# A hybrid decoder layer: the state-space preparation in 21 held phases, later right-hand weights on the way back, the second gate/up stage in program order

## The chip, the cores and the metric

One Trainium2 chip, one core of it. The metric is device microseconds for one execution of the whole layer.

## The reference

One decoder layer on 1024 rows of width 1024, all in float32: half a step of a SwiGLU feed-forward, a mixing layer, another half step of SwiGLU. `D_FF` is 2816, in 22 blocks of 128.

```python
def swiglu(h, w_gate, w_up, w_down):
    return (jax.nn.silu(h @ w_gate) * (h @ w_up)) @ w_down

mod = c_act @ w_ada[l] + b_ada[l]          # 9 vectors of 1024: shift, scale, gate of three sub-layers
h = modulate(rms_norm(x, g_pre_ff1[l]), sh1, sc1)
x = x + 0.5 * ga1 * rms_norm(swiglu(h, w1_gate[l], w1_up[l], w1_down[l]), g_post_ff1[l])
h = modulate(rms_norm(x, g_pre_mix[l]), sh2, sc2)
proj = h @ w_in[l]                         # q, k, v for attention, u for the state-space part
attn = sliding_window_attention(q, k, v, attn_sinks[l])
ssm = s5_ssm(u, ssm_a_re[l], ...)          # powers of lam_bar = exp(dt*lam), B_bar, C: tables from parameters alone
mixed = concat(rms_norm(attn, g_attn_out[l]), rms_norm(ssm, g_ssm_out[l])) @ w_out[l]
x = x + ga2 * rms_norm(mixed, g_post_mix[l])
h = modulate(rms_norm(x, g_pre_ff2[l]), sh3, sc3)
x = x + 0.5 * ga3 * rms_norm(swiglu(h, w2_gate[l], w2_up[l], w2_down[l]), g_post_ff2[l])
```

## The kernel before

Every large product is float32 made of three float32r matmuls (`mm3`, L74 to L76: high by high, high by low, low by high). `split` makes the halves: ScalarE copies the high one (L69), VectorE subtracts for the low one (L70). On top of that the products are Strassen's: sums and differences of quadrants, computed on VectorE, replace one product in eight.

The stages follow each other on TensorE:

- The first gate/up stage (`g1`, to 517 us). It begins with quadrant products whose results are combined in `first_done`; then `rest` runs 140 products of 12 matmuls, seven (1, 5, 6, 2, 7, 3, 4) for each 128-block of the gate or up weights. `rest` converts the weights of the product after the next (`wt.conv(i + 3)`), runs the product (`step`) and calls a hook (`hook1(i)`). After a product ScalarE copies its bank into a buffer `h` (L468, L470, L472) or VectorE adds to one (L464, L456); the fourteenth product of a pair of blocks ends in four sums (`sums`, L427, into four `h` buffers), which are stored in DRAM (`g_d`) for the way back.
- The first way back (`down(0)`, 517 to about 690 us), 66 products of `PRODUCTS` over `NH_F` = 11 blocks: `load` fetches the stored left operand and, for products 1 and 2, the weight pair L and R; `sums` forms differences of weights (L530, L532, L535, L537); `conv` splits both operands. Loads run seven products ahead. Its hook is `hook2(s)`.
- The mixing layer (to about 1040 us), the second gate/up stage (`g2`, to 1517) and the second way back (`down(2)`), the same code as the first two. `g2` computes its `sums` on POOL (GpSimd), `g1` on DVE (VectorE).

A list scheduler with estimated times decides the order of each engine's instructions. Three things bind it: `pinned(f)` chains what `f` issues to the previous pinned instruction of the same engine; `tc.keep_in_program_order` holds one instruction; `g1.rest` gets `pinned`, `g2.rest` gets a function that pins nothing.

Three jobs lie beside the products. The modulation vectors are 72 blocks: a load of 512 KB and one VectorE multiply-and-reduce (`ada_block`, L164, 128x1024; `ada_half`, L169, half of one). 40 of them run in `hook1` until about product 60, 16 halves in `hook2`, 8 in `hook3`. `gate_row` and `gate_store` (L177, L183) turn a vector of gates into a row through TensorE. And the preparation of the state-space part, `prep_steps`, returns 12 steps; `hook1` calls one each at the products of `prep_at`, not pinned; what is left over is called in `hook2`. Its last eight are `step_e` and `step_f` for four q: VectorE rows L1207 to L1215, TensorE transposes L1235 and small products L1270.

## Time and profile before

| | |
|---|---|
| median of 3 runs | 1730.32 us (1730.04 to 1730.64) |
| the profiled execution | 1733.73 us, span 1732.0 us, mean granted clock 0.983 |
| TensorE (PE) busy | 1663.4 us, 96% |
| VectorE (DVE) busy | 1261.8 us, 73% |
| ScalarE (ACT) busy | 813.1 us, 47% |
| GpSimd (POOL) busy | 201.4 us, 12% |
| DMA | 249 MB, mean 144 GB/s |

A group row reads: line, engine, operation, output<-inputs, shapes, xcount, then busy time and mean nanoseconds of one, then the engine's idle time ahead of it and what ended that. A row of waits reads: engine, line that waited <- engine and line waited for: total us, times, longest. A timeline row: start us, duration of the run of like instructions, engine, line, operation, count. A row of a stretch reads: from:to, its length, then busy time (and count) of PE, PE's weight loads, DVE, ACT and POOL, then the clock that TensorE was granted (1 is full), the share of the 16 DMA engines, and GB/s. A busy PE is not PE at its peak: the count in a stretch says more.

### The profile page before, as it was taken

Reading aid. Unit: us, or ns where it says so; the run is one execution under the profiler, and the core shown is the slowest. Engines: PE = TensorE matmul, PEld = TensorE weight load, DVE = VectorE, ACT = ScalarE, POOL = GpSimd, SP = SyncE. Lnnn points to the kernel's source line nnn. Section 1 sums busy time; section 2 is a strip of 40 time slices with the busy share of each in tenths; the row PEclk is TensorE's granted clock in tenths of the full one; section 3 lists DMA queues with packets and bytes.
Section 4 is the critical chain, followed back from the end, with each engine's and each line's share of the span. In section 5 each row is a group of like instructions: output and inputs, shape, how many; then the busy total and the mean of one; then the engine's idle time right before and its main releaser. Section 6 shows DMA issues by size and latency. Waiting matters only on the chain.

```text
span 1732.0 us, 22199 instructions
## 1 busy us (share of the span) xinstructions
PE 1663.4 (96%) x7669; PEld 1358.0 (78%) x7669; DVE 1261.8 (73%) x2426; ACT 813.1 (47%) x1656; POOL 201.4 (12%) x208
## 2 busy tenths in 40 slices
PE   5999999999998999899989998989999999999998
PEld 4878887778886888788767886868888888888886
DVE  7989998995569758826489378785665555687586
ACT  5633335534334457835575257723333333344562
POOL 0011100120010000000013044021211111110001
PEclk8999999999999999999999998999999999999999
DMA  9176742453298342500143126152332223394334
GB/s 377 38 269 228 260 162 104 157 169 105 73 367 281 109 123 101 193 25 25 55 121 94 47 75 197 71 182 101 101 127 98 98 97 109 107 393 139 106 105 160
DMA packets 111041, 249.08 MB, mean 144 GB/s; under 512 B 12088, under 2 KB 27744, under 8 KB 110928
## 3 DMA queue, kind: packets, MB, share of 16 engines
q1 hardware_dynamic: 99776, 209.40, 35.4%
q0 software_dynamic: 10576, 37.21, 6.3%
q8 instruction: 60, 0.98, 0.2%
q10 hardware_dynamic: 576, 1.05, 0.2%
q14 instruction: 53, 0.43, 0.1%
HBM read 187.87 MB, written 59.75 MB: 143 GB/s over the span
## 4 chain that ended last, share of the span: by engine, by line
PE 49%; DVE 6%; issue 1%; ACT 1%; DMA 1%; POOL 0%; DVEq 0%; SPq 0%; ACTq 0%; POOLq 0%
PE b L75 14%; PE b L76 14%; PE b L74 14%; DVE a L70 1%; PE b L743 1%; PE b L831 1%; PE b L833 1%; PE b L832 1%; PE b L777 1%; ACT a L69 1%; PE b L922 0%; PE b L203 0%; DMA w<-in_w_out 0%; DVE w L70 0%; PE b L918 0%
## 5 line engine op out<-in xcount | busy, mean ns | idle before, releaser
L74 PE MATMUL b<-a,w 128*128 128x512 f32 x1260 | 494.0, 396 | 13.6 <-ACT h L468 7.4
L75 PE MATMUL b<-a,w 128*128 128x512 f32 x1260 | 496.3, 394 | 5.2 <-DVE a L70 5.2
L76 PE MATMUL b<-a,w 128*128 128x512 f32 x1260 | 494.1, 395 | 4.7 <-DVE w L70 4.7
L74 PEld LDWEIGHTS b<-a,w 128*128 128x128 f32 x1260 | 240.3, 191 | 67.1 <-ACT h L468 9.6
L76 PEld LDWEIGHTS b<-a,w 128*128 128x128 f32 x1260 | 240.0, 190 | 57.5 <-DVE w L70 6.9
L75 PEld LDWEIGHTS b<-a,w 128*128 128x128 f32 x1260 | 240.1, 191 | 56.5 <-DVE a L70 6.6
L70 DVE TENSOR_TENSOR w<-r,w 128x512 fp32r<-128x512 f32 (+1 forms) x206 | 153.8, 748 | 104.9 <-ACT w L69 103.9
L75 PE MATMUL b<-w,r 128*128 128x512 f32 x528 | 205.1, 391 | 5.9 <-DVE w L70 5.6
L69 ACT CAST w<-r 128x512 fp32r<-128x512 f32 (+1 forms) x210 | 130.5, 625 | 161.7 <-PE b L76 93.6
L76 PE MATMUL b<-w,r 128*128 128x512 f32 x528 | 203.7, 390 | 0.4 <-DVE r L70 0.4
L74 PE MATMUL b<-w,r 128*128 128x512 f32 x528 | 176.5, 390 | 0.8 <-ACT w L69 0.4
L69 ACT CAST r<-a 128x512 fp32r<-128x512 f32 x110 | 68.3, 623 | 151.9 <-PE b L76 84.6
L70 DVE TENSOR_TENSOR r<-a,r 128x512 fp32r<-128x512 f32 x110 | 77.6, 706 | 73.6 <-ACT r L69 72.0
L75 PEld LDWEIGHTS b<-w,r 128*128 128x128 f32 x528 | 99.1, 188 | 30.2 <-DVE w L70 9.7
L464 DVE TENSOR_TENSOR h<-h,b 128x512 f32<-128x512 f32 x120 | 82.1, 686 | 52.9 <-PE b L76 50.3
L74 PEld LDWEIGHTS b<-w,r 128*128 128x128 f32 x528 | 98.9, 188 | 22.2 <-ACT w L69 0.9
L76 PEld LDWEIGHTS b<-w,r 128*128 128x128 f32 x528 | 99.0, 188 | 21.0 <-DVE r L70 0.8
L70 DVE TENSOR_TENSOR w<-t,w 128x512 fp32r<-128x512 f32 (+1 forms) x114 | 79.8, 700 | 47.2 <-ACT w L69 47.1
L427 POOL TENSOR_TENSOR h<-h,h 128x512 f32<-128x512 f32 x44 | 71.0, 1624 | 305.5 <-DVE h L456 303.9
L69 ACT CAST w<-t 128x512 fp32r<-128x512 f32 (+1 forms) x114 | 70.1, 615 | 67.4 <-DVE t L335 28.4
L70 DVE TENSOR_TENSOR w<-a,w 128x512 fp32r<-128x512 f32 x110 | 77.3, 703 | 3.8 <-ACT w L69 3.8
L69 ACT CAST w<-a 128x512 fp32r<-128x512 f32 x110 | 67.9, 618 | 16.4 <-PE b L76 7.2
(378 smaller groups left out, 2586.7 us busy)
## 6 DMA issues: line engine op xcount, KB each, us to landing
r<-in_w_gu SPq DMA_DIRECT2D x88, 512.0 KB, 4.1
g_d<-h SPq DMA_DIRECT2D x154, 256.0 KB, 2.1
a<-g_d SPq DMA_DIRECT2D x110, 256.0 KB, 2.8
q<-in_w_ada POOLq DMA_DIRECT2D x48, 512.0 KB, 4.6
a<-in_w_d SPq DMA_DIRECT2D x88, 256.0 KB, 5.4
a<-in_w_ada SPq DMA_DIRECT2D x16, 512.0 KB, 10.2
a<-in_x SPq DMA_DIRECT2D x12, 512.0 KB, 6.6
x_d<-a SPq DMA_DIRECT2D x12, 512.0 KB, 3.6
```

What stands on the lines that cost most here:

```text
L69: act.copy(hi, src)
L70: eng.tensor_tensor(lo, src, hi.bitcast(F32), op=SUB)
L74: pe.matmul(psum, wh, xh, start=first, stop=False, skip_group_check=goes_on)
L75: pe.matmul(psum, wh, xl, start=False, stop=False, skip_group_check=goes_on)
L76: pe.matmul(psum, wl, xh, start=False, stop=last, skip_group_check=goes_on)
L427: self.eng.tensor_tensor(d, x, y, op=op)
L464: dve.tensor_tensor(dst, dst, pb, op=ADD)
L743: pe.matmul(pb[kv][:, m % 2, ks], qT[m][rows, t * P : (t + 1) * P], kT[rows, (t + 1 - nk) * P : (t + 1) * P], start=True, stop=True,)
L777: pe.transpose(pt[:, m, :], pr[4 * kv + m][:, b * P : (b + 1) * P], ident)
L831: pe.matmul(pb, hh, wh, start=k == 0, stop=False)
L832: pe.matmul(pb, hh, wl, start=False, stop=False)
L833: pe.matmul(pb, hl, wh, start=False, stop=k == NK - 1)
```

## The change

- `pinned` gets `hold`: with `hold=False` an instruction stands behind the pinned ones ahead of it, and later pinned ones need not follow it.
- `prep_steps` becomes `prep_phases`, a generator of 21 phases. `hook1` runs the next phase, pinned with `hold=False`, at each product i with i % 7 in (2, 5) once the modulation blocks are done: products 61, 65, 68 and so on to 131. The first loads and is followed by a pinned `gate_store(0)`; 65 to 79 are the exponentials, angles, powers and kr/bb; 82 to 100 are the turn tables, in three steps each with two sets of buffers; 103 to 131 are e and f, each part's small products a phase behind its VectorE part. What `hook2` would drain is then empty.
- In both ways back the right-hand weights are loaded `LAG` = 4 products later than the left, and their difference (L530) is formed four products later.
- `hook2` begins the late modulation halves at product 26 (loads) and 30 (the reduction), before at 18 and 22; their loads go from POOL's queue to SP's, in program order, as does the load of c.
- `g2.rest` and `hook3` are pinned. `hook3` begins its 8 blocks at products above 8 instead of 3, and stores the gate row at 44 instead of 40.
- `sums` runs on DVE in both gate/up stages. Two single holds in the preparation go.

```diff
-    def pinned(f, *args):
+    def pinned(f, *args, hold=True):
...
-            last_of[i.engine] = i
+            if hold:
+                last_of[i.engine] = i
...
-                self.eng.tensor_tensor(d, x, y, op=op)
+                dve.tensor_tensor(d, x, y, op=op)
...
+    LAG = 4
...
-                    L[i], R[i] = slot(f"a{i}", [2, 512]), slot(f"a{16 + i}", [2, 512])
-                for h, x in enumerate((L, R)):
-                    tc.keep_in_program_order(sp.dma_start(x[i][:, c], wd[i, c, :, h]))
+                    L[i] = slot(f"a{i}", [2, 512])
+                tc.keep_in_program_order(sp.dma_start(L[i][:, c], wd[i, c, :, 0]))
+            if LAG <= s < 2 * NH_F + LAG:
+                c, i = divmod(s - LAG, NH_F)
+                if c == 0:
+                    R[i] = slot(f"a{16 + i}", [2, 512])
+                tc.keep_in_program_order(sp.dma_start(R[i][:, c], wd[i, c, :, 1]))
...
-            if m == "2":
-                dve.tensor_tensor(R[i][:, 0], R[i][:, 1], R[i][:, 0], op=SUB)
-            elif m == "6":
+            k = s - NH_F - LAG
+            if 0 <= k < NH_F:
+                dve.tensor_tensor(R[k][:, 0], R[k][:, 1], R[k][:, 0], op=SUB)
+            if m == "6":
...
-        steps = [step_base, lambda: two(step_tw, 0), lambda: two(step_tw, 2)]
+        yield from step_base()
+        for q in range(6):
+            yield
+            for f, k in ((tw_store, q - 2), (tw_turns, q - 1), (tw_angles, q)):
+                if 0 <= k < 4:
+                    f(k)
         parts = [f(q) for q in range(4) for f in (step_e, step_f)]
-        steps.append(parts[0][0])
-        for i in range(1, 8):
-            steps.append(lambda i=i: (parts[i - 1][1](), parts[i][0]()))
-        steps.append(parts[7][1])
-        return steps
+        for i in range(9):
+            yield
+            if i > 0:
+                parts[i - 1][1]()
+            if i < 8:
+                parts[i][0]()
...
-        elif prep and i == prep_at[0]:
-            prep_at.pop(0)
-            prep.pop(0)()
-            if len(prep_at) == 10:
-                gate_store(0)
+        elif prep and i % 7 in (2, 5):
+            pinned(next, prep[0], None, hold=False)
+            if not stored:
+                pinned(gate_store, 0)
+                stored.append(0)
...
-        elif s >= 2 * NH_F - 4:
+        elif s >= 2 * NH_F + 4:
             if not late_c:
-                late_c.append(load_c(pool))
+                late_c.append(load_c(sp))
...
-                pool.dma_start(w, a["w_ada"][j][:, 512 * h : 512 * h + 512])
+                tc.keep_in_program_order(sp.dma_start(w, a["w_ada"][j][:, 512 * h : 512 * h + 512]))
...
-            if s >= 2 * NH_F and late_raw:
+            if s >= 2 * NH_F + 8 and late_raw:
...
-        if last_raw and i > 3 and i % 2:
+        if last_raw and i > 8 and i % 2:
...
         if i == 40:
             gate_row(2, 8, True)
+        if i == 44:
             gate_store(2)
 
-    g2.rest(hook3, lambda f, *args: f(*args))
+    g2.rest(lambda i: pinned(hook3, i), pinned)
```

The orders that follow are those of one engine. A row is the line, the operation, output<-inputs and the shape; the lines of the changed kernel are 2 higher from L113 on, 8 higher from L526 on and 14 to 16 higher in the preparation (L169 is L171 there, L183 L185, L427 L429, L464 L466, L530 L538, L1207 L1221, L1270 L1284).

VectorE in `g1.rest`, before, ahead of the converted weight (`w_430`) of about product 86, where four sums stand among preparation rows (L1207 to L1210 of e or f, L1291 and L1292 of the turn tables):

```order
L335 TENSOR_TENSOR t_428_2807<-r_400_2594,r_399_2592 128x512
L1291 TENSOR_SCALAR q_418_2723<-q_417_2722 128x512
L1208 TENSOR_TENSOR q_440_2887<-q_355_2151,q_356_2152 128x512
L456 TENSOR_TENSOR h_404_2645<-h_404_2645,b_406_2650 128x512
L1292 TENSOR_TENSOR q_417_2722<-q_417_2722,q_418_2723 128x512
L427 TENSOR_TENSOR h_412_2699<-h_381_2486,h_404_2645 128x512
L427 TENSOR_TENSOR h_407_2663<-h_404_2645,h_384_2505 128x512
L427 TENSOR_TENSOR h_410_2682<-h_407_2663,h_381_2486 128x512
L1207 TENSOR_TENSOR q_438_2885<-q_355_2151,q_356_2152 128x512
L1210 TENSOR_TENSOR q_439_2886<-q_355_2151,q_356_2152 128x512
L427 TENSOR_TENSOR h_429_2822<-h_386_2522,h_410_2682 128x512
L70 TENSOR_TENSOR w_430_2831<-t_428_2807,w_430_2831 128x512
```

The changed kernel's VectorE ahead of the converted weight of product 114 (`w_509`), with rows of the phase at 110 (L1221 to L1229) and the four sums behind product 111 (L429). From the row behind the converted weight of 112 to this one there are 18 rows, of which these are the last 12; the first of the 18 is the last that needs nothing of product 110:

```order
L70 TENSOR_TENSOR w_506_3408<-r_471_3176,w_506_3408 128x512
L337 TENSOR_TENSOR t_507_3411<-r_472_3178,r_471_3176 128x512
L1293 SCALAR_TENSOR_TENSOR c_502_3395<-delta,cols,c_502_3395 128x16
L458 TENSOR_TENSOR h_479_3238<-h_479_3238,b_481_3243 128x512
L1223 TENSOR_TENSOR q_503_3399<-q_503_3399,q_505_3401 128x512
L429 TENSOR_TENSOR h_487_3292<-h_461_3111,h_479_3238 128x512
L429 TENSOR_TENSOR h_482_3256<-h_479_3238,h_464_3130 128x512
L1225 TENSOR_TENSOR q_505_3401<-q_356_2169,q_357_2170 128x512
L429 TENSOR_TENSOR h_485_3275<-h_482_3256,h_461_3111 128x512
L1229 TENSOR_TENSOR q_504_3400<-q_504_3400,q_505_3401 128x512
L429 TENSOR_TENSOR h_508_3426<-h_466_3147,h_485_3275 128x512
L70 TENSOR_TENSOR w_509_3435<-t_507_3411,w_509_3435 128x512
```

The turn-table rows are gone from among the sums, and rows of one part are left there.

VectorE at the start of the first way back, before (L169 are the modulation halves, each with a readout row):

```order
L70 TENSOR_TENSOR w_661_4309<-a_643_4214,w_661_4309 128x512
L169 ISA h_708_4609,modc<-h_708_4609,c_707_4606,cols 128x512
L169 ISA modc 128x1
L169 ISA h_709_4611,modc<-h_709_4611,c_707_4606,modc 128x512
L169 ISA modc 128x1
L70 TENSOR_TENSOR r_666_4352<-a_648_4224,r_666_4352 128x512
L169 ISA h_710_4613,modc<-h_710_4613,c_707_4606,cols 128x512
L169 ISA modc 128x1
L70 TENSOR_TENSOR w_667_4353<-a_649_4226,w_667_4353 128x512
L169 ISA h_711_4615,modc<-h_711_4615,c_707_4606,modc 128x512
L169 ISA modc 128x1
L70 TENSOR_TENSOR r_669_4375<-a_653_4248,r_669_4375 128x512
```

And in the changed kernel, the splits there (of `r` the left operand, of `w` the weights) and the first sums:

```order
L70 TENSOR_TENSOR w_669_4389<-a_605_4114,w_669_4389 128x512
L70 TENSOR_TENSOR r_675_4418<-a_653_4282,r_675_4418 128x512
L70 TENSOR_TENSOR w_676_4419<-a_607_4118,w_676_4419 128x512
L538 TENSOR_TENSOR a_612_4128<-a_612_4128 128x512
L540 TENSOR_TENSOR a_601_4104<-a_601_4104,a_612_4128 128x512
L543 TENSOR_TENSOR t_748_4874<-a_612_4128,a_601_4104 128x512
```

No half stands among these splits. Some twenty products on:

```order
L70 TENSOR_TENSOR w_740_4812<-a_635_4202,w_740_4812 128x512
L171 ISA h_732_4781,modc<-h_732_4781,c_731_4778,cols 128x512
L171 ISA modc 128x1
L70 TENSOR_TENSOR r_742_4832<-a_721_4701,r_742_4832 128x512
L171 ISA h_733_4783,modc<-h_733_4783,c_731_4778,modc 128x512
L171 ISA modc 128x1
L70 TENSOR_TENSOR w_743_4833<-a_638_4208,w_743_4833 128x512
L171 ISA h_734_4785,modc<-h_734_4785,c_731_4778,cols 128x512
L171 ISA modc 128x1
L70 TENSOR_TENSOR r_745_4853<-a_724_4722,r_745_4853 128x512
```

Here the halves come one per product among the splits.

VectorE at the start of `g2`'s products, before, from the last combination of first results (L411) on; L164 are modulation blocks:

```order
L411 TENSOR_TENSOR h_1693_9827<-h_1693_9827,b_1669_9655 128x512
L411 TENSOR_TENSOR h_1694_9830<-h_1694_9830,b_1670_9659 128x512
L70 TENSOR_TENSOR a_1700_9849<-q_1508_8845,a_1700_9849 128x512
L70 TENSOR_TENSOR a_1705_9864<-q_1513_8850,a_1705_9864 128x512
L70 TENSOR_TENSOR a_1701_9852<-q_1509_8846,a_1701_9852 128x512
L70 TENSOR_TENSOR w_1684_9736<-t_1683_9734,w_1684_9736 128x512
L164 ISA q_1710_9888,modc<-q_1710_9888,c_1709_9885,cols 128x1024
L164 ISA modc 128x1
L70 TENSOR_TENSOR a_1702_9855<-q_1510_8847,a_1702_9855 128x512
```

And in the changed kernel, from the same combination (L413 there) on:

```order
L413 TENSOR_TENSOR h_1690_9826<-h_1690_9826,b_1666_9655 128x512
L70 TENSOR_TENSOR a_1696_9845<-q_1504_8841,a_1696_9845 128x512
L70 TENSOR_TENSOR a_1701_9860<-q_1509_8846,a_1701_9860 128x512
L70 TENSOR_TENSOR a_1697_9848<-q_1505_8842,a_1697_9848 128x512
L70 TENSOR_TENSOR a_1698_9851<-q_1506_8843,a_1698_9851 128x512
L70 TENSOR_TENSOR w_1680_9732<-t_1679_9730,w_1680_9732 128x512
L70 TENSOR_TENSOR a_1702_9863<-q_1510_8847,a_1702_9863 128x512
L429 TENSOR_TENSOR h_1693_9832<-h_1675_9715,h_1689_9823 128x512
L429 TENSOR_TENSOR h_1691_9830<-h_1689_9823,h_1690_9826 128x512
L429 TENSOR_TENSOR h_1692_9831<-h_1691_9830,h_1675_9715 128x512
L429 TENSOR_TENSOR h_1694_9833<-h_1676_9719,h_1692_9831 128x512
```

The blocks are gone from there, and the four sums that POOL ran before are in the row.

TensorE in `g2`, before, where the gate row's transpose (L183) stands within the third block's products:

```order
L76 MATMUL b_1707_9870<-a_1702_9855,w_1716_9913 128x512
L76 MATMUL b_1714_9898<-a_1706_9867,w_1718_9930 128x512
L183 MATMUL b_1814_10687<-ident,ggc 8x128
L74 MATMUL b_1732_10033<-a_1685_9740,w_1724_9989 128x512
L75 MATMUL b_1732_10033<-a_1685_9740,w_1724_9989 128x512
```

And in the changed kernel:

```order
L75 MATMUL b_1814_10713<-a_1688_9771,w_1813_10710 128x512
L76 MATMUL b_1814_10713<-a_1688_9771,w_1813_10710 128x512
L185 MATMUL b_1821_10764<-ident,ggc 8x128
L74 MATMUL b_1823_10772<-a_1649_9541,w_1816_10728 128x512
L75 MATMUL b_1823_10772<-a_1649_9541,w_1816_10728 128x512
```

It stands some 450 rows later, behind a whole product.

## The prediction

> **What bounds the kernel now.** I began with the page: engine shares, then the chain that ended last, then stretches of 40 us, and only then the waits inside the stretches where TensorE was not full.

> ```profile
> PE 1663.4 (96%) x7669; PEld 1358.0 (78%) x7669; DVE 1261.8 (73%) x2426; ACT 813.1 (47%) x1656; POOL 201.4 (12%) x208
> PE 49%; DVE 6%; issue 1%; ACT 1%; DMA 1%; POOL 0%; DVEq 0%; SPq 0%; ACTq 0%; POOLq 0%
> 400.00:440.00 40.00, 40.00 (x178) 33.15 (x177) 24.99 (x38) 14.17 (x26) 0.00 (x0) 1.00 0.28 99
> 280.00:320.00 40.00, 38.64 (x168) 31.09 (x168) 35.50 (x67) 26.52 (x61) 3.17 (x5) 1.00 0.40 138
> 320.00:360.00 40.00, 38.48 (x189) 29.57 (x188) 36.97 (x60) 16.55 (x31) 8.83 (x15) 0.96 0.37 130
> 360.00:400.00 40.00, 37.95 (x191) 29.76 (x190) 30.55 (x50) 15.63 (x29) 8.90 (x12) 0.96 0.50 166
> 480.00:520.00 40.00, 39.56 (x175) 32.41 (x174) 27.03 (x47) 15.54 (x27) 6.45 (x12) 1.00 1.02 378
> 520.00:560.00 40.00, 34.32 (x140) 25.11 (x139) 40.00 (x79) 17.34 (x31) 2.15 (x4) 1.00 0.81 281
> 560.00:600.00 40.00, 39.08 (x173) 32.04 (x172) 30.36 (x50) 18.00 (x32) 0.00 (x0) 1.00 0.38 119
> 1120.00:1160.00 40.00, 32.63 (x127) 25.11 (x126) 35.33 (x51) 14.56 (x27) 9.98 (x13) 0.91 0.55 191
> ```

> TensorE is the bound: 96% busy and half of the final chain, DVE 6%. No fewer products are computed after the change, so it can only win where TensorE is not full. The first number of each stretch is its length, then PE's busy time with its count. The yardstick is 400–440: 178 matmuls of 512 columns in 40 us, 0.2247 us each. A stretch's loss is the number missing from 178, times 0.2247. Three places of the change lose much:

> - 280–400, where the state-space preparation runs now;
> - 480–600, the start of the first way back: 175 + 140 + 173 = 488 of 534, 46 missing, 10.3 us;
> - 1120–1160, the start of the second gate/up stage: 127 of 178, 51 missing, 11.5 us.

> In the first, small products hide the count, so they are taken out:

> ```profile
> L76 PE MATMUL b<-a,w 128*128 128x512 f32 x150 | 60.8, 405 | 2.0 <-DVE w L70 2.0
> L74 PE MATMUL b<-a,w 128*128 128x512 f32 x150 | 60.8, 405 | 2.5 <-ACT h L468 2.5
> L75 PE MATMUL b<-a,w 128*128 128x512 f32 x150 | 59.6, 397 | 0.0
> L1235 PE MATMUL b<-ident,q 128*128 128x128 f32 x32 | 4.8, 272 | 0.0
> L1270 PE MATMUL b<-q,q 128*32 128x128 f32 x64 | 3.9, 280 | 0.4 <-DVE q L1213 0.4
> ```

> There are 450 large ones; the 96 small ones have a quarter of the columns, worth 24. 534 − 450 − 24 = 60 missing: 13.5 us. Of these the windows show 1.36 + 1.52 + 2.05 = 4.9 idle and two drops of the clock (0.96 twice: 0.04 × 40 = 1.6 us each), 3.2. The other 5.4 us lie around the small products, which stand singly between matmuls of a large product.

> **Place 1, the 21 phases.** Nothing is removed; DVE's preparation rows go from a bunch to seven products' worth of time per two phases (products 61 to 131, some 230 to 465 us). DVE issues one row of 512 every 0.60 us:

> ```profile
> 83.34 1.89 DVE L70 TENSOR_TENSOR a<-q,a 128x512 fp32r<-128x512 f32 x3
> 85.14 0.68 DVE L411 TENSOR_TENSOR h<-h,b 128x512 f32<-128x512 f32 x1
> 85.74 0.68 DVE L70 TENSOR_TENSOR a<-q,a 128x512 fp32r<-128x512 f32 x1
> 86.34 0.68 DVE L411 TENSOR_TENSOR h<-h,b 128x512 f32<-128x512 f32 x1
> ...
> 88.15 1.29 DVE L70 TENSOR_TENSOR a<-q,a 128x512 fp32r<-128x512 f32 x2
> 89.35 2.74 DVE L427 TENSOR_TENSOR h<-h,h 128x512 f32<-128x512 f32 x4
> 120.00:160.00 40.00, 40.00 (x179) 33.10 (x178) 37.20 (x59) 13.79 (x24) 5.30 (x10) 1.00 0.72 247
> ```

> Per seven products (19.0 us of PE) DVE has 18 rows of its own, 10.9 us, and in the heaviest phases an e and an f part of 6 rows each, 3.6 and 4.0: 18.5 us, 97%, less the small products' own PE time. That is near the 120–160 stretch, where DVE is 93% busy and PE still full. So the mean load passes; the peak is the risk. Every fourteenth product ends in four L427 sums ahead of the next converted weight. With a phase at 110 and the sums behind 111, the rows from behind the converted weight of 112 to that of 114 are 18, one of them a 0.2 us one: 10.4 us. They begin with what product 110 leaves; from its end to the start of 114 TensorE has three products, 8.2 us: 2.2 us short; the same again at 128, and some 0.4 at 100. By the same count before has 10.0 us of rows ahead of about product 72, 1.9 short, and the trace shows 1.4 idle (280–320). At that ratio I take 1.7 + 1.7 + 0.4 = 3.8 us of stalls, and one clock drop, 1.6. The small products now stand in blocks at a product's end: of the 5.4 us around them between nothing and all may go; I keep 3.0, since the blocks still switch shapes four times each. After: 8.4. Gain 13.5 − 8.4 = **5.1** (0 if peaks and switches cost what they do now; 11 if neither stalls). In a phase ACT's angles and POOL's stores are off the path: ACT is 16 of 40 us busy there. gate_store(0) waits only for a gate row finished at product 60.

> **Place 2, the first way back.** Six waits there are for a split weight behind a full DVE:

> ```profile
> PE b L75 <- DVE w L70: 5.6, 6, 1.3
> L169 DVE CUSTOM_DVE_ANT_0 h<-h,c,modc 128x512 f32<-128x512 f32 x8 | 6.0, 745 | 0.0
> L169 DVE CUSTOM_DVE_ANT_0 h<-h,c,cols 128x512 f32<-128x512 f32 x8 | 6.0, 744 | 0.0
> L530 DVE TENSOR_TENSOR a<-a 128x512 f32<-128x512 f32 x11 | 7.5, 684 | 0.4 <-DMA a<-in_w_d 0.4
> 1520.00:1560.00 40.00, 40.00 (x178) 33.14 (x177) 35.08 (x52) 20.01 (x36) 4.17 (x3) 1.00 1.05 392
> 600.00:640.00 40.00, 40.00 (x178) 33.14 (x177) 20.67 (x33) 19.71 (x35) 0.00 (x0) 1.00 0.43 130
> ```

> The change takes the 16 L169 halves (16 × 0.67 issued = 10.7 us of DVE) out of it, spreads L530 by four products, and puts the halves at products 30 to 45. The second way back (1520–1560) has the same sums and splits without the halves, with the DMA engines at 1.05: PE loses nothing, DVE 35. So the loss of 520–600 goes and the 0.7 of 480–520 (3 missing, at the stage's turn) stays: **9.6** (7 if a third of the waits is the raw weights', 10.3 at most). The halves' new cover: at 600–640 DVE is 20.7 of 40 and PE full; 16 halves over 16 products (43 us) make it 31. The right-hand loads come four products later but still seven ahead of use, 19 us against 5.4 to landing on the page, so they cost nothing; without that lead each late pair would cost up to 5.4. The halves' 16 loads move from POOL's queue into SP's, in program order. Behind one that waits for its buffer stand the next products' loads, and TensorE after 19 us of that; the buffer is free once the half eight before is done, so I take 0.

> **Place 3, the second gate/up stage.**

> ```profile
> PE b L183 <- DVE ggc L177: 3.5, 1, 3.5
> PE b L74 <- ACT h L468: 2.4, 1, 2.4
> PE b L76 <- DVE w L70: 1.2, 1, 1.2
> L164 DVE CUSTOM_DVE_ANT_0 q<-q,c,cols 128x1024 f32<-128x1024 f32 x8 | 11.5, 1449 | 0.0
> 1126.78 2.54 POOL L427 TENSOR_TENSOR h<-h,h 128x512 f32<-128x512 f32 x2
> 1131.93 1.27 POOL L427 TENSOR_TENSOR h<-h,h 128x512 f32<-128x512 f32 x1
> 1127.05 4.04 DVE L70 TENSOR_TENSOR a<-q,a 128x512 fp32r<-128x512 f32 x3
> PE b L74 <- ACT h L468: 2.5, 1, 2.5
> 80.00:120.00 40.00, 37.51 (x166) 30.74 (x165) 34.03 (x55) 16.62 (x30) 6.57 (x12) 1.00 0.64 223
> ```

> (The last wait row and window are the first gate/up stage's.) The 8 L164 blocks, bunched here, spread from product 9 on; the gate row that TensorE waited 3.5 us for goes to products 40 and 44, when its blocks are long done; and the sums that now run on POOL, beside which three DVE rows took 4.04 us instead of 1.9, go to DVE. What stays is the third product's wait for a buffer that the sums free. The first stage has this order already, sums on DVE, and waits 2.5 us; there four rows stand between the second L411 and the sums, here six: 2 × 0.6 more, 3.7. Pinning also stops TensorE from taking other products meanwhile. With one clock drop (the 0.91 is two: 0.09 × 40 / 2 = 1.8) after is 5.5, gain **6.0** (2.5 if all six rows add to the wait, and two drops; 9 with the first stage's 2.5 and no drop). The 44 sums add 44 × 0.60 = 26 us to DVE over 360 us, where DVE is 22 of 40 (1160–1200): nothing on the path.

> ```profile
> 1160.00:1200.00 40.00, 40.00 (x178) 33.10 (x177) 22.24 (x33) 14.77 (x27) 5.90 (x4) 1.00 0.28 99
> 690.00:1040.00 350.00, 336.32 (x1768) 270.43 (x1767) 221.46 (x537) 188.10 (x490) 44.70 (x42) 0.98 0.26 82
> ```

> Between the stages the same rows come in a slightly other order; the 13.7 us that PE idles there may move by a fifth either way: 0, ±3.

> **Sum.** 5.1 + 9.6 + 6.0 = 20.7. The profiled execution took 1733.73, so 1713.0 of such a one; the median of runs is 3.4 lower, 1730.3, and the forecast 1730.3 − 20.7 = 1709.6. All low ends (0, 7, 2.5, −3) give 1724; all high ends 1697.

> [...] The waits at 326 were 0.5 and 1.0 us, and the 320–360 window shows 0.96; the first stage waited 2.5 us at a granted 1.00. So short waits sometimes cost a drop here and sometimes not, and I count one at place 1 and one at place 3. [...]

> **Rivals.**

> A. The peaks of place 1 eat their gain: DVE lags at 100, 114 and 128 by the full count (2.2 + 2.2 + 0.4), with a drop each (4.8 in all) and the small products cost 4. 13.5 us again, 1730.3 − 15.6 = 1714.7. For it: 97% DVE in the e/f phases. Against: the count overstates by a third at product 72. 0.15.

> B. At g2's start pinning lets TensorE stand for all six rows, 6.1, with two drops: gain 1.8, so 1713.8. For: no other product may overtake. Against: the first stage. 0.12.

> C. None of the forecast stalls brings a drop of the clock: 1730.3 − 20.7 − 3.4 = 1706.2. For: 2.5 us at 1.00 in the first stage. Against: 0.96 after 1.0. 0.12.

> D, slower: the e and f blocks are pinned in TensorE's order behind a DVE chain. If DVE is a whole part late, TensorE waits for it mid-way: 3.8 us and a drop of 1.6 at each of nine phases, 49 us where 13.5 are lost now: +35 − 15.6 = 1749. It decides from the sixth such phase on (29.1 / 5.4). Against: a block stands a phase behind its chain, three or four products, 8 to 11 us, and the largest backlog counted is 2.2. 0.05.

> E. The waits only move: what leaves 520–560 turns up at the halves' new place, and the phases' as in A: gain 0 to 3. Against: DVE 20.7 of 40. 0.04.

> **Chances.** The forecast's own case 0.52. A measurement tells about 0.2%, 3.5 us. Faster A + B + C + own = 0.91, same E 0.04, slower D 0.05. Range 1700 to 1722: low ends of places 1 and 3 together (1730.3 − 9.6 − 2.5 = 1718) and −3 of the middle above, C with place 1 free of stalls below.

> **What would show it.** Right: 178 matmuls in the 40 us from the first way back's second window; no wait for L177's gate row; one wait of 3 to 5 us for the h copy at the second stage's start; DVE near 37 of 40 over products 103 to 131 with two waits of 1 to 2 us at its fourteenth products. Wrong: waits at every e or f block, a wait for DMA in products 26 to 45 of the first way back, a drop of the clock at each stall.

## The result and the profile after

The changed kernel takes 1718.54 us, median of 4 runs (1716.62 to 1720.42), beside 1730.48 us of the kernel before: ratio 0.9927, 95% interval 0.9909 to 0.9944. That is 11.9 us of the 20.7 forecast. Its profiled execution took 1718.82 us, so the two profiled executions differ by 14.9.

The page's engine row, and then the stretches of 40 us at the three places:

```profile
PE 1652.9 (96%) x7669; PEld 1355.8 (79%) x7669; DVE 1264.6 (74%) x2470; ACT 804.3 (47%) x1654; POOL 124.8 (7%) x147
280.00:320.00 40.00, 40.00 (x178) 33.10 (x177) 34.39 (x121) 16.33 (x34) 0.90 (x2) 1.00 0.28 99
320.00:360.00 40.00, 38.87 (x170) 31.35 (x169) 32.34 (x54) 25.34 (x57) 1.63 (x3) 1.00 0.39 139
360.00:400.00 40.00, 39.86 (x191) 32.09 (x190) 33.55 (x56) 16.49 (x30) 4.93 (x9) 1.00 0.43 145
400.00:440.00 40.00, 39.20 (x204) 31.24 (x203) 35.86 (x59) 15.43 (x29) 6.70 (x11) 1.00 0.44 151
480.00:520.00 40.00, 40.00 (x178) 33.14 (x177) 28.38 (x47) 18.34 (x33) 0.00 (x0) 1.00 1.03 375
520.00:560.00 40.00, 40.00 (x179) 33.10 (x178) 36.61 (x63) 17.30 (x31) 0.00 (x0) 1.00 0.54 168
560.00:600.00 40.00, 40.00 (x178) 33.14 (x177) 32.68 (x64) 19.93 (x37) 0.00 (x0) 1.00 0.70 225
600.00:640.00 40.00, 38.87 (x172) 31.87 (x171) 27.22 (x46) 22.97 (x40) 0.00 (x0) 1.00 0.42 130
1120.00:1160.00 40.00, 38.09 (x161) 31.36 (x162) 26.41 (x41) 14.62 (x25) 1.06 (x2) 0.96 0.46 161
```

The first 120 us of the way back are dense (178, 179, 178), where 46 matmuls were missing; the second gate/up stage's start has 161 of 178, before 127. The preparation's stretch shows no clock below 1.00. What TensorE still waits for, by the waits of products 85 to 130, of the way back from product 26 on, and of the second stage's start:

```profile
PE b L74 <- ACT h L470: 2.2, 3, 1.1
PE b L76 <- DVE w L70: 0.4, 1, 0.4
PE b L75 <- DVE w L70: 1.1, 1, 1.1
PE b L74 <- ACT h L470: 4.3, 1, 4.3
```

The wait of 3.5 us for the gate row is gone. The stages in between paid for part of this. I cut the trace at the same counts of TensorE's 7669 instructions in every kernel, those at 240, 480, 660, 1100 and 1200 us in before. In each part I summed what the starts lie apart beyond the usual interval of that line and shape, the median in before for all kernels (0.227 us for 512 columns). Loss in us (places 1 to 3 are the parts from 240, 480 and 1100 us; the column 660–1100 is the turn after the first way back to the second gate/up stage's first products):

| profiled execution | first 240 us | place 1 | place 2 | 660–1100 | place 3 | rest | sum |
|---|---|---|---|---|---|---|---|
| before | 17.7 | 13.8 | 10.5 | 30.6 | 11.5 | −0.8 | 83.3 |
| changed | 18.2 | 7.6 | 1.2 | 34.5 | 7.0 | −0.6 | 67.8 |
| e5, the changed kernel again | 18.3 | 7.6 | 1.7 | 34.0 | 7.0 | −0.6 | 67.9 |
| e1, phases alone | 17.5 | 7.5 | 10.5 | 30.1 | 11.4 | −0.8 | 76.3 |
| e2, way back alone | 17.5 | 12.2 | 4.9 | 31.4 | 9.9 | −0.8 | 75.3 |
| e3, gate/up alone | 18.3 | 10.4 | 8.8 | 29.8 | 6.1 | −0.6 | 72.7 |
| e6, all but the way back | 18.5 | 7.6 | 8.8 | 30.5 | 6.3 | −0.6 | 71.2 |
| e7, all but the phases | 17.3 | 12.1 | 3.7 | 32.0 | 7.9 | −0.6 | 72.4 |
| e8, all but the gate/up | 18.2 | 7.5 | 1.7 | 33.7 | 9.5 | −0.8 | 69.9 |

The three places won 6.2 + 9.3 + 4.5 = 20.0 us; the stages between lost 3.9, the beginning 0.5.

### The profile page after: what moved, and what is told of

Same layout as the page of the kernel before. It is cut to its first block, busy times and chain, and to the rows that moved or that the text cites. A ratio compares the mean times of both kernels' runs of the same rounds, so it can differ in the third digit from the quotient of the medians.

```text
span 1717.0 us, 22221 instructions
## 1 busy us (share of the span) xinstructions
PE 1652.9 (96%) x7669; PEld 1355.8 (79%) x7669; DVE 1264.6 (74%) x2470; ACT 804.3 (47%) x1654; POOL 124.8 (7%) x147
## 3 DMA queue, kind: packets, MB, share of 16 engines
q10 hardware_dynamic: 576, 1.05, 0.2%
## 4 chain that ended last, share of the span: by engine, by line
PE 51%; DVE 4%; DMA 2%; ACT 1%; issue 1%; POOL 1%; SPq 0%; DVEq 0%; ACTq 0%; POOLq 0%
PE b L76 15%; PE b L75 15%; PE b L74 15%; PE b L751 1%; PE b L839 1%; PE b L841 1%; PE b L840 1%; PE b L785 1%; DMA r<-in_w_gu 1%; PE b L930 0%; PE b L205 0%; DMA w<-in_w_out 0%; ACT a L69 0%; POOL a L913 0%; PE b L926 0%
## 5 line engine op out<-in xcount | busy, mean ns | idle before, releaser
L74 PE MATMUL b<-a,w 128*128 128x512 f32 x1260 | 489.3, 393 | 15.1 <-ACT h L470 9.0
L75 PE MATMUL b<-a,w 128*128 128x512 f32 x1260 | 494.6, 392 | 5.6 <-DVE a L70 5.6
L76 PE MATMUL b<-a,w 128*128 128x512 f32 x1260 | 494.5, 392 | 1.4 <-DVE w L70 1.3
L74 PEld LDWEIGHTS b<-a,w 128*128 128x128 f32 x1260 | 238.0, 189 | 68.6 <-ACT h L470 11.5
L75 PEld LDWEIGHTS b<-a,w 128*128 128x128 f32 x1260 | 238.5, 189 | 56.3 <-DVE a L70 7.0
L76 PEld LDWEIGHTS b<-a,w 128*128 128x128 f32 x1260 | 238.6, 189 | 53.6 <-DVE w L70 3.8
L70 DVE TENSOR_TENSOR w<-r,w 128x512 fp32r<-128x512 f32 (+1 forms) x206 | 142.9, 694 | 137.9 <-ACT w L69 137.6
L75 PE MATMUL b<-w,r 128*128 128x512 f32 x528 | 205.5, 389 | 1.1 <-DVE w L70 1.1
L76 PE MATMUL b<-w,r 128*128 128x512 f32 x528 | 205.4, 389 | 0.0
L74 PE MATMUL b<-w,r 128*128 128x512 f32 x528 | 180.7, 389 | 0.0
L70 DVE TENSOR_TENSOR r<-a,r 128x512 fp32r<-128x512 f32 x110 | 75.7, 688 | 61.7 <-ACT r L69 61.6
L75 PEld LDWEIGHTS b<-w,r 128*128 128x128 f32 x528 | 99.1, 188 | 22.2 <-DVE w L70 1.6
L74 PEld LDWEIGHTS b<-w,r 128*128 128x128 f32 x528 | 99.1, 188 | 20.6
L76 PEld LDWEIGHTS b<-w,r 128*128 128x128 f32 x528 | 99.1, 188 | 20.5
L69 ACT CAST w<-t 128x512 fp32r<-128x512 f32 (+1 forms) x114 | 69.9, 613 | 83.7 <-DVE t L337 30.4
L70 DVE TENSOR_TENSOR w<-t,w 128x512 fp32r<-128x512 f32 (+1 forms) x114 | 79.7, 699 | 31.5 <-ACT w L69 31.3
L466 DVE TENSOR_TENSOR h<-h,b 128x512 f32<-128x512 f32 x120 | 82.2, 685 | 21.3 <-PE b L76 19.2
L454 ACT ACTIVATE h<-h 128x512 f32<-128x512 f32 x60 | 38.0, 633 | 117.8 <-DVE h L466 117.8
L70 DVE TENSOR_TENSOR w<-a,w 128x512 fp32r<-128x512 f32 x110 | 75.3, 685 | 0.2 <-ACT w L69 0.2
L74 PE MATMUL b<-a,a 128*128 128x512 f32 x182 | 72.2, 399 | 0.1
## 6 DMA issues: line engine op xcount, KB each, us to landing
a<-in_w_ada SPq DMA_DIRECT2D x16, 512.0 KB, 10.2
```

The source lines that it names most:

```text
L69: act.copy(hi, src)
L70: eng.tensor_tensor(lo, src, hi.bitcast(F32), op=SUB)
L74: pe.matmul(psum, wh, xh, start=first, stop=False, skip_group_check=goes_on)
L75: pe.matmul(psum, wh, xl, start=False, stop=False, skip_group_check=goes_on)
L76: pe.matmul(psum, wl, xh, start=False, stop=last, skip_group_check=goes_on)
L454: act.activation(dst, src, AF.Silu)
```

## The experiments

**Each part alone.** Each is the kernel before with one part of the change: e1 with `prep_phases`, `hold` and `hook1`; e2 with the loads, `LAG` and `hook2`; e3 with the second stage pinned, its blocks later and its sums on DVE. The line of each that decides, in this order:

```diff
+            pinned(next, prep[0], None, hold=False)
...
+    LAG = 4
...
+            if s >= 2 * NH_F + 8 and late_raw:
...
+                dve.tensor_tensor(d, x, y, op=op)
+    g2.rest(lambda i: pinned(hook3, i), pinned)
```

> The kernel before with the 21 held phases alone. Theory (the three places add up; the mixing layer is worse only because the way back's part of the change reorders it): the stages between the first way back and the second gate/up stage keep before's order and loss; place 1 saves what the changed kernel shows there, about 6 us, so 1724 (ratio 0.9964). Rival (the mixing layer's extra loss follows from any shift of what runs ahead of it): TensorE loses about 5 us more there than before, and the kernel comes out near 1729.

> The kernel before with the later right-hand weights and the later modulation halves alone. Theory: the first way back saves about 9 us and the mixing layer, in the changed kernel's order, loses about 5 more, so 1726. Rival (the mixing layer's loss is a matter of the run, not of the order): 1721.

> The kernel before with the second gate/up stage pinned, its sums on VectorE and its blocks later, alone. Theory: 5 us saved in 1080 to 1200 and nothing elsewhere, 1725. Rival (the mixing layer is reordered by this part too): near 1730.

Beside 1732.42 us of before on their chip they took 1728.82 (ratio 0.9980, 0.9964 to 0.9995), 1727.55 (0.9972, 0.9960 to 0.9984) and 1726.29 (0.9956, 0.9941 to 0.9971). The ratios' gains add to 0.92%, the whole change's was 0.73% (e5: 0.84%), within the intervals: the parts add as far as the noise lets one see. The table's column 660–1100 tells the theories apart: with e1 and e3 it is no more than before (30.1, 29.8), with e2 0.8 us more. VectorE's rows there stand in e1, e3 and e6 exactly as in before, in e2, e7 and e8 exactly as in the changed kernel. So it is the way back's part that reorders the mixing layer.

e2's gain is below the theory's 9 at its own place for another reason: place 2 won 5.6 there and not 9.3. TensorE waited 3.3 us at the halves' new place, 1.1 in the changed kernel, and then ran at half clock (granted 0.50) for 3.41 us, from 610.0 us on:

```profile
PE b L75 <- DVE w L70: 3.3, 1, 3.3
600.00:640.00 40.00, 36.69 (x155) 29.97 (x154) 22.69 (x39) 19.48 (x35) 0.00 (x0) 0.96 0.55 171
```

e1's median gain of 3.6 us is below the 6 expected. The 6 came from before's profile, and that had two half-clock stretches of 3.41 us at place 1 (at 326 and 374 us). e2's and e7's profiles have one, e3's has none, with the same preparation and the same waits (2.5 and 2.0 us). Their losses at place 1 are 13.8 with two, 12.2 and 12.1 with one and 10.4 with none: each stretch costs some 1.7 us. e3 was to save 5 us at place 3 and nothing elsewhere. It saves 5.4 there; its trace has 5.1 less loss at places 1 and 2 as well, which its edit does not touch.

**All but one part**, with the changed kernel again (e5) on the same chip: e6, e7 and e8 have before's lines in place of those of e2, e1 and e3.

```diff
-    LAG = 4
...
-            if s >= 2 * NH_F + 8 and late_raw:
+            if s >= 2 * NH_F and late_raw:
...
-            pinned(next, prep[0], None, hold=False)
...
-    g2.rest(lambda i: pinned(hook3, i), pinned)
+    g2.rest(hook3, lambda f, *args: f(*args))
```

> The changed kernel itself once more, beside the three that follow. Theory (the places save 6, 9 and 5 us, the mixing layer and chance drops of the clock give some 6 back): 12 to 14 us faster than before. Rival (its first measurement had unlucky drops): 18 or more.

> The changed kernel with the way back (loads, LAG, halves, their queue) as before; its mixing layer has then before's order on every engine. Theory (the new order costs the mixing layer 4 to 5 us): the first way back loses 9 us again and the mixing layer regains 4 to 5, so 4 to 5 us slower than the changed kernel. Rival (the order costs nothing): 9 us slower.

> The changed kernel with the preparation in its 12 steps as before. Theory: 6 us slower than the changed kernel, the mixing layer unchanged. Rival (what leaves place 1 comes back elsewhere in the changed kernel): the same time.

> The changed kernel with the second gate/up stage not pinned, its sums on GpSimd and its blocks as before. Theory: 5 us slower than the changed kernel, all of it at 1080 to 1200. Rival: the waits there depend on what ran ahead, and less than 2.

Beside 1734.53 of before: e5 1719.13 (0.9916, 0.9894 to 0.9938), e6 1726.47 (0.9965, 0.9946 to 0.9984), e7 1725.43 (0.9945, 0.9924 to 0.9965), e8 1722.26 (0.9936, 0.9911 to 0.9961). e5's gain of 15.4 us lies between theory and rival. e7 is 6.3 slower than e5, as its theory has it, and every run of e7 (from 1721.77 on) lies above every run of e5 (to 1720.12). e8 is 3.1 slower, between its theory's 5 and its rival's 2. Place 1 loses 7.5 or 7.6 with the phases in every kernel, 10.4 to 13.8 without. e6 is 7.3 slower, between the 4 to 5 of the theory and the rival's 9. Its table row speaks more clearly: its mixing layer, in before's order, loses 30.5. In this column the five kernels with the way back's part (changed, e2, e5, e7, e8) have 31.4 to 34.5, mean 33.1; the four without (before, e1, e3, e6) 29.8 to 30.6, mean 30.3. The ranges don't touch: 2.8 us. The waits show where. TensorE's waits in the attention and scan part, first before's (860 to 920 us), then the changed kernel's:

```profile
PE b L74 <- ACT h L69: 2.4, 2, 1.9
PE b L75 <- DVE h L70: 2.0, 2, 1.0
PE b L798 <- DVE t L796: 0.9, 1, 0.9
```

```profile
PE b L75 <- DVE h L70: 5.2, 1, 5.2
PE b L888 <- ACT r L802: 2.1, 1, 2.1
PE b L806 <- DVE t L804: 1.8, 1, 1.8
PE b L785 <- DVE a L900: 1.0, 1, 1.0
```

5.3 us became 10.1. The wait of 5.2 is there in all five kernels with the way back's part, word for word, and in none of the other four. By the table's measure, cut at the same counts, this part loses 14.4 us in the changed kernel and 10.7 in before: 3.7 us. VectorE's rows ahead of the wait of 5.2 in the changed kernel, and GpSimd's beside them:

```profile
885.78 0.73 DVE L915 TENSOR_TENSOR a<-a,a 128x508 f32<-128x508 f32 x1
886.43 2.70 DVE L774 TENSOR_SCALAR a<-a,s 128x256 f32<-128x256 f32 x2
889.05 1.01 DVE L774 TENSOR_SCALAR c<-c,s 128x256 f32<-128x256 f32 x2
889.98 0.60 DVE L774 TENSOR_SCALAR a<-a,s 128x256 f32<-128x256 f32 x2
890.51 0.60 DVE L774 TENSOR_SCALAR c<-c,s 128x256 f32<-128x256 f32 x2
891.03 0.68 DVE L897 TENSOR_TENSOR a<-b,q 128x512 f32<-128x512 f32 x1
891.63 0.68 DVE L70 TENSOR_TENSOR h<-b,h 128x512 fp32r<-128x512 f32 x1
...
885.93 1.71 POOL L914 TENSOR_TENSOR a<-a,q 128x512 f32<-128x512 f32 x1
887.72 1.26 POOL L915 TENSOR_TENSOR a<-a 128x508 f32<-128x508 f32 x1
```

The split that TensorE needs (L70) stands behind eight scalings of the softmax (L774), two of which took 2.70 us beside GpSimd's rows, later ones 0.60. In before the first split stood right behind the scan's products:

```profile
898.71 0.68 DVE L906 TENSOR_TENSOR a<-a,q 128x512 f32<-128x512 f32 x1
899.31 0.68 DVE L70 TENSOR_TENSOR h<-b,h 128x512 fp32r<-128x512 f32 x1
...
900.02 0.64 DVE L70 TENSOR_TENSOR h<-b,h 128x512 fp32r<-128x512 f32 x1
```

Nothing in the diff touches these rows. The scheduler, which orders by estimated times, put them otherwise because the stage ahead had changed. **Which detail of it?** In e4 the halves' loads go back to POOL's queue and are no longer held in program order; the order of VectorE in the mixing layer is then nearly before's, that of ScalarE less so:

```diff
-                tc.keep_in_program_order(sp.dma_start(w, a["w_ada"][j][:, 512 * h : 512 * h + 512]))
+                pool.dma_start(w, a["w_ada"][j][:, 512 * h : 512 * h + 512])
```

> The changed kernel with the loads of the late modulation halves back on GpSimd's queue and not held; the mixing layer's VectorE and ScalarE order is then that of before, and the halves stand at products 25 to 45 as in the changed kernel. Theory (the order is the cause): the mixing layer loses some 30 us as before instead of 35, 1713.5. Rival (run or position, not order): as the changed kernel, 1718.5.

It took 1720.05 us, ratio 0.9920 (0.9896 to 0.9944): no faster than the changed kernel. Its waits there are before's again,

```profile
PE b L74 <- ACT h L69: 2.4, 2, 1.9
PE b L75 <- DVE h L70: 1.7, 2, 1.0
PE b L806 <- DVE t L804: 0.9, 1, 0.9
870.00:910.00 40.00, 35.02 (x165) 25.85 (x163) 33.81 (x72) 21.22 (x57) 5.95 (x5) 0.69 0.21 66
```

and yet only 165 instructions went through in the 40 us, at a granted clock of 0.69: in this execution TensorE ran at half clock for 30.7 us from 885.5 on, in before for 6.8. Its runs spread from 1715.78 to 1725.05 with mean clocks of 0.984 to 0.979, the lower clocks with the longer times. The attention and scan part loses 20.9 us in e4, of which half clock alone took 15.4. It loses 13.5 to 17.7 in the eight kernels with the wait of 5.2 (e11, e13 and e14 below have it too) and 9.8 to 10.8 in the five others with about before's waits (before, e1, e3, e6, e9). That the halves' loads, by their queue or by the hold that goes with it, set the order, and the order the waits, is shown; what it is worth in time, e4 leaves open.

**Parts of parts.** Three more of the changed kernel's decisions, and one thing that it leaves.

```diff
-                dve.tensor_tensor(d, x, y, op=op)
+                self.eng.tensor_tensor(d, x, y, op=op)
```

> The changed kernel with the second gate/up stage's sums back on GpSimd, pinned. Theory (pinned, the third product waits for all four sums, 1.6 us each there and 0.6 on VectorE): 4 us more wait at the stage's start, 3 to 5 us slower than the changed kernel. Rival (the pinning alone does it): the same time as the changed kernel.

It took 1731.12, ratio 1.0006 (0.9991 to 1.0021): the whole gain is gone, 12 us against 3 to 5 expected. Its profiled execution is the slowest of its 12 (1739.05), so its losses are on the high side. Place 3 lost 13.7 instead of 7.0, and the rest of the stage and the last way back, dense in all kernels above, 5.0; place 2, which the edit leaves alone, lost 6.4 with 6.83 us at half clock. The waits of the whole stage, then its sums on GpSimd:

```profile
PE b L74 <- ACT h L470: 8.1, 10, 2.6
L429 POOL TENSOR_TENSOR h<-h,h x44: 1260/1292/2254, 1122.0 to 1527.8; 128x512 f32<-128x512 f32 x44
```

Ten waits, one for each pair of blocks. Without pinning the scheduler could put other work between; pinned, TensorE waits for the 1.3 us sums. With the sums on VectorE (0.69 us each) TensorE waits for the first four alone. Taken alone, neither half of the gate/up part is what it is with the other:

```diff
-        if last_raw and i > 8 and i % 2:
+        if last_raw and i > 3 and i % 2:
...
-    g2.rest(lambda i: pinned(hook3, i), pinned)
+    g2.rest(hook3, lambda f, *args: f(*args))
```

> The changed kernel with the second gate/up stage and its hook not pinned and the blocks as before, the sums on VectorE. Theory (the blocks bunched at the start and the gate row early were most of the loss): 3 to 5 us slower than the changed kernel, with a wait for the gate row. Rival (GpSimd's sums were): the same time.

1724.65, ratio 0.9950 (0.9936 to 0.9964). Place 3 lost 13.4 us, as much as with GpSimd's sums; 6.8 of them are half clock, and this execution (1727.11) is the slowest of five. The wait is another than expected: not the gate row, but a weight split behind the eight blocks (10.2 us of VectorE) and the sums that are now beside them:

```profile
PE b L76 <- DVE w L70: 4.5, 1, 4.5
PE b L74 <- ACT h L470: 2.6, 1, 2.6
PE b L74 <- ACT h L474: 0.7, 1, 0.7
```

```diff
-                tc.keep_in_program_order(sp.dma_start(L[i][:, c], wd[i, c, :, 0]))
...
+                for h, x in enumerate((L, R)):
+                    tc.keep_in_program_order(sp.dma_start(x[i][:, c], wd[i, c, :, h]))
```

> The changed kernel with both right-hand weights loaded together with the left as before (no LAG), the late halves as changed. Theory (the halves on VectorE were the first way back's loss): the same there within 1 us, under 2 missing matmuls in its first 120 us. Rival (the DMA engines, full at the start, were): 5 us or more lost there again.

1724.90, ratio 0.9957 (0.9944 to 0.9971), by the ratios 5 to 7 us slower than the changed kernel. Place 2 lost 3.6, nothing of it in the first 120 us, so the theory holds there: the halves were the loss, not the full DMA engines (their share at 480 to 520 us was 1.02 in before, and 1.03 in the changed kernel, where TensorE was full). The 3.6 lie at the halves' new place, where TensorE waited 2.0 us and a half-clock stretch of 3.41 followed. The mixing layer and place 3 lose 34.9 and 8.4 in the table's columns, with a third order.

**The buffers turned by two.** The stage's first copies wait for a buffer that the third and fourth sum still read.

```diff
                     self.sums(0, [slot(o_rot(), [512]) for _ in range(4)])
+                o_rot.i += 2
```

> The changed kernel with the rotation of the eight h buffers moved on by two after the first four results and their sums in each gate/up stage. The first two copies of the stage then go into buffers that the second of the four sums frees, not the third and fourth; the mixing layer's order also falls back to nearly that of before. Theory (the wait at each gate/up stage's start is for the last of the four sums, and the mixing layer's order costs 4 us): 1.2 us less wait at about 92 and at about 1122 us, 4 us less in the mixing layer, 6 less than the changed kernel, ratio to before near 0.988. Rival (the wait is for VectorE's rows ahead of all sums): the waits stay at 2.5 and 4.3.

1714.38 us (1713.08 to 1718.41), ratio 0.9900 (0.9883 to 0.9916). The changed kernel had 0.9927 (0.9909 to 0.9944) and, as e5, 0.9916 on two other chips: 3 to 5 us in e9's favour, but the intervals overlap. Its waits at the start of the first stage, of the second, and in the attention part:

```profile
PE b L74 <- ACT h L475: 2.5, 1, 2.5
PE b L74 <- ACT h L471: 1.8, 1, 1.8
...
PE b L74 <- ACT h L471: 3.1, 1, 3.1
...
PE b L74 <- ACT h L69: 2.1, 2, 1.9
PE b L75 <- DVE h L70: 1.8, 1, 1.8
```

The second stage waits 1.2 us less, as the theory has it; the first 0.7 less, but a later copy (L475) now waits 2.5. The mixing layer is back at before's waits: its column is 25.9, 8.6 less than the changed kernel's, of which 2.1 are lost again in the first 240 us and 2.7 in the way back. So what its profile has over the changed kernel's came by the mixing layer's order and clock, and only 1.6 at place 3 by the buffers.

## Why the prediction was right, and where not

The direction and the range held; the predicted gain, 20.7 us, was too large: 11.9 on the first chip, 15.4 on e5's.

- **Place 1: 5.1 forecast, 6.2 measured.** Two waits stand where the count put them, at the fourteenth products (from 402.6 and 445.9 us on), and are smaller: 0.8 (in two parts) and 0.7, not 1.7 each; VectorE is 35.9 of 40 busy there. One of 1.1 at 342, among the turn tables, was not forecast. No drop of the clock came. The small products cost 5 us as before and not 3: 7.6 lost less 2.6 of waits. The errors nearly cancelled, and luck is in the 6.2: before's profile had both its drops there, 3.4 us. Against the 10.4 of e3, which had none with the same preparation, the phases win 2.8. Rival A would have left 13.5 there, against 7.5 or 7.6 in every kernel with the phases; rival D needed six long waits.
- **Place 2: 9.6 forecast, 9.3 measured.** The part costed at nothing was the halves' new place: TensorE waited 1.1 us there. VectorE, with a split behind it, stood for a half whose load had not landed:

```profile
DVE h L171 <- DMA h<-in_w_ada: 4.3, 4, 1.5
```

  I had looked for a blocked SP queue behind the loads, not for their own lateness among the stored operands' loads. A wait for DMA in products 26 to 45 was a named sign of being wrong, and it came, on VectorE. The 9.3 is a good case: in e2, e7, e9 and e13 TensorE waited 2.0 to 3.3 us there with a drop of the clock behind it, and place 2 won 5.6 to 6.9.
- **Place 3: 6.0 forecast, 4.5 measured.** The wait was 4.3, forecast 3.7, with one drop of the clock as forecast; 0.4 more came later. Rival B, 6.1, did not come. The prediction prices B's case twice, as a low end of 2.5 and as 1.8; two drops and a wait of 6.1 leave 1.8 of 11.5.
- **The mixing layer: 0 ± 3 forecast, −3.9 measured** (mean over the kernels −2.8). This is the step that failed, in its mechanism more than in its size: "the same rows come in a slightly other order; the 13.7 us that PE idles there may move by a fifth either way". I took the share of the rows that moved, not which: eight scalings on VectorE ahead of one split made TensorE wait 5.2 us, and the part around it lost 3.7 us more.
- **The median.** The profiled execution of before was 3.4 us above the median, that of the changed kernel at it, so 3 of the 14.9 us are not in the medians of the first chip. On e5's chip the medians differ by 15.4, so chance is as large as that.
- **The clock.** I counted two drops at the three places; one came, at place 3 behind the wait of 4.3. Rival C, no drop and 1706 us, did not come.

## What to carry to other kernels

Where a scheduler orders unpinned rows by estimated times, an edit in one stage reorders the next; compare the order of all stages and price what now stands ahead of each critical split. When an engine's program is pinned, a producer that was only hidden by overtaking becomes a wait, as the sums on GpSimd did in e11 (ten waits, 8.1 us): move the slow ones first. A loss read from one profile also holds what the clock did in that execution (3.4 us at place 1 here): read it in several. Where two edits share an engine, test each without the other: sums on VectorE and pinning were worth nothing or less apart.

## What the runs showed of the hardware

The same wait of 2.5 us at the first gate/up stage's start (about 92 us) came with a drop of the clock in some kernels and not in others. Two kernels, same code there (e3, then e7):

```profile
80.00:120.00 40.00, 37.51 (x159) 30.55 (x158) 33.14 (x54) 16.63 (x30) 6.54 (x12) 0.96 0.62 217
80.00:120.00 40.00, 37.51 (x166) 30.75 (x165) 34.03 (x56) 16.79 (x31) 6.54 (x12) 1.00 0.66 223
```

The 1.52 us are two waits close together, of 0.5 and 1.0. The grid lies otherwise in the two profiles; what sets it was not tried. The same wait cost some 1.6 us more in one execution than in another (159 and 166 matmuls in the two rows above, 0.227 us each). The spread between runs goes with the clock: before took 1727.65 us at a mean clock of 0.985 and 1743.08 at 0.978 on one chip.
